# A reciprocal root moved from VectorE to GpSimd, and smaller first stores, in a two-layer decoder trunk

## The chip, the cores and the metric

The kernel runs on one core of one Trainium2 chip. Its engines work side by side, each through a queue of its own and in that queue's order: TensorE (PE) multiplies matrices, VectorE (DVE) and ScalarE (ACT) work elementwise, GpSimd (POOL) is a set of programmable cores, and SyncE (SP) issues transfers. Transfers between the core's SBUF and the chip's memory run on sixteen DMA engines. Matrix products land in PSUM, from where VectorE or ScalarE fetch them. The metric is the device time of one execution in microseconds (us), as the median of several runs.

## The reference

The model is a causal decoder trunk with two layers, 256 positions and a width of 2048, all in float32. Layer 0 mixes positions with eight stick-breaking heads and eight dilated-window heads, layer 1 with sixteen forgetting-attention heads. Each layer then has a gated feed-forward block with a depthwise convolution of width three (5632 columns per half), and a gated per-layer embedding. What matters here is the norm, which stands ahead of each mixer, of each feed-forward block and of each gate, and once more at the end, seven in all:

```python
def rmsnorm(x, g):
    x32 = x.astype(jnp.float32)
    y = x32 * lax.rsqrt(jnp.mean(x32 * x32, axis=-1, keepdims=True) + RMS_EPS)
    return (y * g.astype(jnp.float32)).astype(x.dtype)

def reference(...):
    h = x
    for i in range(DEPTH):
        a = rmsnorm(h, attn_norm[i])
        ...  # h = h + mixer(a)
        h = h + conv_ffn(rmsnorm(h, ffn_norm[i]), w_up[i], conv_w[i], conv_b[i], w_down[i])
        gate = jax.nn.sigmoid(rmsnorm(h, ple_norm[i]) @ w_ple_gate[i])
        h = h + gate * (p[i] @ w_ple[i])
    return rmsnorm(h, final_norm)
```

So for each of the 256 positions one number is needed, the reciprocal root of the mean square over 2048 features.

## The kernel before

The hidden state `h` stays in SBUF, features on the 128 partitions: 16 blocks of 128 features by 256 positions. Activations are held as two float32r parts (a rounded value and its rest), and so are the weights. A weight product is three matmuls (`PARTS`: high by high, high by low, low by high). Weights stream in from memory in groups of up to 1 MB over SyncE's queue (`issue_group`, L149) into three raw buffers. `split_unit` makes the two parts of one unit: ScalarE rounds (L165), VectorE subtracts (L166). Four such split buffers exist, and `LOOK = 3` units are kept ready ahead of TensorE. A unit is typically 4 blocks of 128 by 256 columns, 24 matmuls.

A counter of units used, the tick, orders what is done beside the matmuls: `defer(n, fn)` puts `fn` off until n units later. `norm_finish` defers `norm_sums` by 3 ticks and `norm_rows` by 5, so that two units of matmuls stand between them in TensorE's queue. What uses the norm's rows is put off until then as well (`with_rows`). The order within each engine's queue is finally laid out by a planner when the program is built: it takes the order of the program as the priority and its own estimates of durations, and may put a ready instruction ahead of one that waits. So in the profile a weight subtraction (L166) can stand among the small operations of a norm.

The norm works in three steps:

1. As each block of `h` is final, its squares are added up into `acc` (L278 to L282).
2. `norm_sums`: the two halves of `acc` are added (L287), four tiny matmuls with a vector of ones sum over the partitions (L291, into `nps`), with positions now on the partitions, two columns of 128. VectorE scales by 1/2048 and adds epsilon (`nv`, L296). Then come twelve operations on 128x2 values (L298 to L306): the reciprocal root by a shift of the bits, a subtraction from a constant, and three Newton steps. The last one writes `rT`.
3. `norm_rows`: `rT` is put on the diagonal of two 128x128 matrices (`nd`, L314, one VectorE operation for each column), which are split into two parts (`ndh` on ScalarE, L321; `ndl` on VectorE, L322) and multiplied with ones by TensorE (`rps`, L324), so that each partition gets the row of 256 roots. VectorE copies it to `rb` (L325), and to `rq` with the attention's scale where a mixer follows.

The columns are applied after the products: an attention's queries and keys, the feed-forward's up-products and the gate's product are multiplied by `rb` or `rq` when they are fetched from PSUM. Values use `rT` as a scale per position.

The seventh norm has no product behind it. The last gate column's product is made in two halves (L716) with their squares in `more` (L727); then come `norm_sums(more)`, `norm_rows(None)`, which multiplies in full float32 without the split (L316), eight products of `h` with the row (L739, 512 columns each, the second operand in PSUM) and, behind each one, a store of 256 KB on SyncE's queue (L740).

GpSimd has nearly nothing to do: four fills that the framework puts at the start and four small loads (the gains `gn` at L359, and L383 to L385).

## Time and profile before

| | before |
|---|---|
| median of 3 runs | 2437.97 us (2437.55 to 2438.04) |
| the profiled execution's own time | 2438.14 us |
| its span (first to last instruction) | 2436.3 us |
| granted TensorE clock, mean | 0.997 of full |
| TensorE busy | 2414.1 us, 99% |
| VectorE busy | 1595.7 us, 65% |
| ScalarE busy | 1228.3 us, 50% |
| GpSimd busy | 2.5 us |
| read from and written to memory | 452.86 MB, 2.10 MB |

Times in the views count from the start of the span. A row of the timeline or of the chain of waits gives start, duration, engine, line and operation, with the output ahead of the arrow and the inputs behind it; x8 means that eight alike are merged, and the brackets at the end of a timeline row hold the engine's idle time before it and what ended that. A row of a grouped view gives the busy time of the group, the mean duration of one in nanoseconds, and the idle time ahead of the group. A row of a table by stretches gives the stretch, the busy time of the five engines, the granted TensorE clock, the DMA engines' busy share and GB/s.

### The profile page before, as it was taken

The numbers are of one execution on the slowest core, as the hardware profiler recorded it, in microseconds if no ns is written. First come the engines' busy times: TensorE is split into PE (matmuls) and PEld (weight loads), VectorE is DVE, ScalarE is ACT, GpSimd is POOL, SyncE is SP. The second block draws the span as 40 slices with busy tenths as digits, with TensorE's granted clock in tenths as the row PEclk, the third lists the DMA queues.
The fourth block names the chain that finished last, engine by engine and source line by source line (L and its number), as shares of the span: only waits on it lengthen the run. The fifth ranks groups of instructions, "written<-read, shape, count | busy, mean of one in ns | idle before, by whom it ended". The sixth has DMA issues, their size and how long they took to land.

```text
span 2436.3 us, 48002 instructions
## 1 busy us (share of the span) xinstructions
PE 2414.1 (99%) x20990; PEld 2400.5 (99%) x20990; DVE 1595.7 (65%) x2157; ACT 1228.3 (50%) x1548; POOL 2.5 (0%) x8
## 2 busy tenths in 40 slices
PE   8999999999999999999999999999999999999997
PEld 8999999999999999999999999999999999999997
DVE  7557666776567657767765555677765776567676
ACT  6554455555355445555554444555543554455553
POOL 0000000000000000000000000000000000000000
PEclk9999999999999999999999999999999999999998
DMA  7444445555555555555554444555555555555553
GB/s 268 169 177 173 169 177 191 194 197 198 190 191 192 188 208 190 191 185 203 187 184 170 165 169 165 190 191 192 195 198 194 191 192 189 203 195 186 189 198 120
DMA packets 66483, 458.06 MB, mean 188 GB/s; under 512 B 7408, under 2 KB 7424, under 8 KB 16608
## 3 DMA queue, kind: packets, MB, share of 16 engines
q1 hardware_dynamic: 66096, 454.53, 52.8%
q8 instruction: 164, 2.69, 0.4%
q0 software_dynamic: 176, 0.46, 0.1%
q14 instruction: 47, 0.39, 0.0%
HBM read 452.86 MB, written 2.10 MB: 187 GB/s over the span
## 4 chain that ended last, share of the span: by engine, by line
PE 97%; DVE 1%; DMA 1%; ACT 1%; issue 0%; SPq 0%; DVEq 0%; ACTq 0%
PE psu L203 39%; PE psd L203 20%; PE pso L203 7%; PE psk L203 7%; PE psv L237 7%; PE psq L203 7%; PE psg L203 7%; DMA wr<-in_w 1%; PE avp L520 1%; PE psp L203 0%; PE pse L716 0%; PE scs L469 0%; PE psv L250 0%; PE sps L511 0%; PE avp L522 0%; PE scs L467 0%
## 5 line engine op out<-in xcount | busy, mean ns | idle before, releaser
L166 DVE TENSOR_TENSOR w<-wr,w 128x1024 fp32r<-128x1024 f32 (+2 forms) x882 | 1051.4, 1193 | 701.2 <-ACT w L165 695.5
L165 ACT CAST w<-wr 128x1024 fp32r<-128x1024 f32 (+2 forms) x882 | 905.6, 1028 | 1082.5 <-PE psu L203 355.1
L203 PE MATMUL psu<-act,w 128*128 128x256 f32 x8448 | 959.3, 276 | 0.0
L203 PEld LDWEIGHTS psu<-act,w 128*128 128x128 f32 x8448 | 958.3, 188 | 0.0
L203 PE MATMUL psd<-act,w 128*128 128x256 f32 x4224 | 479.7, 276 | 0.0
L203 PEld LDWEIGHTS psd<-act,w 128*128 128x128 f32 x4224 | 479.2, 188 | 0.0
L203 PE MATMUL psq<-act,w 128*128 128x256 f32 x1536 | 185.2, 279 | 1.2 <-DVE w L166 1.0
L203 PEld LDWEIGHTS psq<-act,w 128*128 128x128 f32 x1536 | 179.8, 188 | 2.1 <-DVE w L166 1.5
L203 PE MATMUL psk<-act,w 128*128 128x256 f32 x1536 | 180.0, 277 | 0.0
L203 PEld LDWEIGHTS psk<-act,w 128*128 128x128 f32 x1536 | 176.7, 188 | 0.0
L203 PE MATMUL pso<-act,w 128*128 128x256 f32 x1536 | 175.8, 277 | 0.0
L203 PEld LDWEIGHTS pso<-act,w 128*128 128x128 f32 x1536 | 174.9, 188 | 0.0
L237 PE MATMUL psv<-w,act 128*128 128x256 f32 x1440 | 172.7, 279 | 0.0
L237 PEld LDWEIGHTS psv<-w,act 128*128 128x128 f32 x1440 | 168.4, 188 | 1.1
L203 PE MATMUL psg<-act,w 128*128 128x256 f32 x1440 | 164.4, 276 | 0.0
L203 PEld LDWEIGHTS psg<-act,w 128*128 128x128 f32 x1440 | 163.7, 188 | 0.0
L616 DVE TENSOR_TENSOR u<-psu,rb 128x512 f32<-128x512 f32 x88 | 60.8, 691 | 33.3 <-PE psu L203 33.2
L622 DVE SCALAR_TENSOR_TENSOR yg<-u,cv,yg 128x256 f32<-128x256 f32 x176 | 73.3, 477 | 0.0
L622 DVE SCALAR_TENSOR_TENSOR yv<-u,cv,yv 128x256 f32<-128x256 f32 x176 | 73.3, 477 | 0.0
L619 ACT ACTIVATE yg<-u,cv 128x256 f32<-128x256 f32 x88 | 48.0, 594 | 1.0 <-DVE u L616 1.0
L619 ACT ACTIVATE yv<-u,cv 128x256 f32<-128x256 f32 x88 | 48.0, 593 | 0.0
L261 ACT CAST act<-yg 128x512 fp32r<-128x512 f32 x44 | 27.3, 621 | 39.1 <-DVE yg L632 39.1
(173 smaller groups left out, 886.5 us busy)
## 6 DMA issues: line engine op xcount, KB each, us to landing
wr<-in_w SPq DMA_DIRECT2D x388, 1024.0 KB, 4.8
wr<-in_w SPq DMA_DIRECT2D x36, 768.0 KB, 4.3
wr<-in_w SPq DMA_DIRECT2D x8, 896.0 KB, 4.6
wr<-in_w SPq DMA_DIRECT2D x7, 512.0 KB, 6.9
h<-in_x SPq DMA_DIRECT2D x4, 512.0 KB, 7.1
out_dram<-h SPq DMA_DIRECT2D x8, 256.0 KB, 2.4
wr<-in_w SPq DMA_DIRECT2D x2, 816.0 KB, 4.6
ct<-in_c SPq DMA_DIRECT2D x1, 841.0 KB, 6.6
```

The source lines that it names most:

```text
L165: nc.scalar.copy(out=w[:, :, 0, :], in_=raw)
L166: nc.vector.tensor_sub(out=w[:, :, 1, :], in0=raw, in1=w[:, :, 0, :].bitcast(F32))
L203: nc.tensor.matmul(ps[:, j, :], lhsT=w[:, k, s, js], rhs=act[:, k0 - koff + k, t, :], start=first and j + k + n == 0, stop=last and k == k ...
L237: nc.tensor.matmul(ps[:, t], lhsT=act[:, 4 * i + k, a, tsl], rhs=w[:, k, b], start=i + t + k + n == 0, stop=i == 3 and k == kc - 1 and n = ...
L261: nc.scalar.copy(out=dst[:, :, 0, :], in_=src)
L520: nc.tensor.matmul(av[:, 0, j * S:(j + 1) * S], lhsT=v[:, 0, js], rhs=w[:, j * S:(j + 1) * S], start=j == 0, stop=False, skip_group_check= ...
L616: nc.vector.tensor_mul(out=u[:, :, 2:], in0=ps, in1=rb2)
L619: nc.scalar.activation(out=y[:, j, :], in_=u[:, j, 2:], func=AF.Identity, bias=cv[:, l, t, 3:4], scale=cv[:, l, t, 2:3])
L622: nc.vector.scalar_tensor_tensor(out=y[:, j, :], in0=u[:, j, tap:tap + S], scalar=cv[:, l, t, tap:tap + 1], in1=y[:, j, :], op0=ALU.mult, ...
```

## The change

Three edits. The twelve operations behind `nv` become one instruction on GpSimd, a power with the exponent -0.5, which lies in a small constant tile that GpSimd fills at the start. In `norm_rows`, the second of the two diagonal matrices is made by ScalarE, as a copy with a scale, where VectorE made both. And the eight products and stores at the end become nine: two of one block (256 columns, 128 KB), then seven of two blocks (512 columns, 256 KB).

```diff
+    root = cpool.tile([P, 2], F32, name="root")
+    nc.gpsimd.memset(root, -0.5)
...
         v = work.tile([P, 2], F32, name="nv", tag="nv")
-        y = work.tile([P, 2], I32, name="ny", tag="ny")
-        t = work.tile([P, 2], F32, name="nt", tag="nt")
         nc.vector.tensor_scalar(out=v, in0=ps[:, :, 0], scalar1=1.0 / D, scalar2=EPS,
                                 op0=ALU.mult, op1=ALU.add)
-        nc.vector.tensor_single_scalar(out=y, in_=v.bitcast(I32), scalar=1, op=ALU.logical_shift_right)
-        nc.vector.tensor_scalar(out=y, in0=y, scalar1=-1.0, scalar2=float(0x5F3759DF),
-                                op0=ALU.mult, op1=ALU.add)
-        nc.vector.tensor_scalar_mul(out=v, in0=v, scalar1=-0.5)
-        y = y.bitcast(F32)
-        for i in range(3):
-            nc.vector.tensor_mul(out=t, in0=y, in1=y)
-            nc.vector.tensor_mul(out=t, in0=t, in1=v)
-            nc.vector.scalar_tensor_tensor(out=rT if i == 2 else y, in0=t, scalar=1.5, in1=y,
-                                           op0=ALU.add, op1=ALU.mult)
+        nc.gpsimd.tensor_tensor(out=rT, in0=v, in1=root, op=ALU.pow)
...
         for t in range(2):
-            nc.vector.tensor_scalar_mul(out=dg[:, t, :], in0=ident, scalar1=rT[:, t:t + 1])
+            if t == 0:
+                nc.vector.tensor_scalar_mul(out=dg[:, t, :], in0=ident, scalar1=rT[:, t:t + 1])
+            else:
+                nc.scalar.activation(out=dg[:, t, :], in_=ident, func=AF.Copy, scale=rT[:, t:t + 1])
...
-    rps = norm_rows(None).unsqueeze(1).to_broadcast([P, 2, S])
-    for op in range(8):
-        hs = h[:, 2 * op:2 * op + 2, :]
-        nc.vector.tensor_mul(out=hs, in0=hs, in1=rps)
-        nc.sync.dma_start(out=out[:, 2 * op:2 * op + 2, :], in_=hs)
+    rps = norm_rows(None)
+    for k0, k1 in ((0, 1), (1, 2), *((k, k + 2) for k in range(2, KT, 2))):
+        hs = h[:, k0:k1, :]
+        nc.vector.tensor_mul(out=hs, in0=hs, in1=rps.unsqueeze(1).to_broadcast([P, k1 - k0, S]))
+        nc.sync.dma_start(out=out[:, k0:k1, :], in_=hs)
```

## The prediction

> **What bounds the kernel now.** I read the first page first: busy shares, then the chain that ended last.
>
> ```profile
> span 2436.3 us, 48002 instructions
> PE 2414.1 (99%) x20990; PEld 2400.5 (99%) x20990; DVE 1595.7 (65%) x2157; ACT 1228.3 (50%) x1548; POOL 2.5 (0%) x8
> ...
> PE 97%; DVE 1%; DMA 1%; ACT 1%; issue 0%; SPq 0%; DVEq 0%; ACTq 0%
> ```
>
> TensorE is busy for 2414.1 of 2436.3 us, so 22.2 us are all that an edit beside the matmuls can touch. VectorE's 65% is not a limit: taking operations from it pays only where TensorE, or the end, waits for one of them. Two views find such places. The chain of waits, narrowed to the last microseconds, shows the seventh norm, behind which no matmul hides anything:
>
> ```profile
> 2422.98 0.62 PE nps L291 x4
> ...
> 2423.62 0.17 DVE nv L296
> ...
> 2423.82 0.18 DVE ny L298
> ...
> 2425.79 0.17 DVE rT L306
> ...
> 2425.98 0.30 DVE nd L314
> ...
> 2426.32 1.23 PE rps L316 x4
> ...
> 2427.58 0.69 DVE h L739
> ```
>
> From the end of `nv` (2423.62 + 0.17 = 2423.79) to the start of `nd` (2425.98) the chain is twelve small VectorE operations one behind the other: 2.19 us, all on the path that sets the end.
>
> For the six other norms I took TensorE's instructions grouped by line, whose last column is the idle time ahead of the group, and then the timeline of the first norm:
>
> ```profile
> L324 PE MATMUL rps<-ndh,trir 128*128 128x256 f32 x6 | 1.9, 313 | 1.0 <-ACT ndh L321 1.0
> ```
>
> ```profile
> 36.41 6.13 PE L203 MATMUL psk<-act,w 128*128 128x256 f32 x50
> ...
> 38.04 0.15 DVE L296 TENSOR_SCALAR nv<-nps 128x2 f32<-128x2 f32 x1
> ...
> 42.23 0.16 DVE L306 SCALAR_TENSOR_TENSOR rT<-nt,ny 128x2 f32<-128x2 f32 x1
> 42.42 0.48 DVE L314 TENSOR_SCALAR nd<-ct,rT 128x128 f32<-128x128 f32 x2
> ...
> 42.94 0.40 ACT L321 CAST ndh<-nd 128x256 fp32r<-128x256 f32 x1 [0.96 <-DVE nd L314]
> ...
> 43.40 0.39 PE L324 MATMUL rps<-ndh,trir 128*128 128x256 f32 x1 [0.86 <-ACT ndh L321]
> ```
>
> The six together let TensorE wait 1.0 us, and 0.86 of it is the first norm: TensorE was through with its keys at 42.54 (36.41 + 6.13) and got `ndh` at 43.40. The fourth norm has the rest, and the third stands for those without a wait:
>
> ```profile
> 1219.66 4.36 PE L250 MATMUL psv<-w,act 128*128 128x272 f32 x33
> 1219.84 0.16 DVE L296 TENSOR_SCALAR nv<-nps 128x2 f32<-128x2 f32 x1 [0.70 <-PE nps L291]
> ...
> 1224.20 0.39 PE L324 MATMUL rps<-ndh,trir 128*128 128x256 f32 x1 [0.17 <-ACT ndh L321]
> ```
>
> ```profile
> 1133.25 0.16 DVE L296 TENSOR_SCALAR nv<-nps 128x2 f32<-128x2 f32 x1 [0.70 <-PE nps L291]
> ...
> 1138.62 0.28 PE L324 MATMUL rps<-ndh,trir 128*128 128x256 f32 x1
> ```
>
> There the root has 5.2 us between `nv` (1133.41) and the row matmul, which stands two weight units later in TensorE's queue. So the change can win at three places only: 2.19 us at the end, 0.86 and 0.17 in the middle.
>
> **The power itself.** It takes the place of twelve operations seven times, and one wait of VectorE on itself becomes a wait for GpSimd and one back. The trace has no arithmetic on GpSimd; the nearest rows are these, with an exponential of ScalarE for the function:
>
> ```profile
> L359 POOL DMA_DIRECT2D gn<-in_g x1 | 0.7, 668 | 0.8 <-POOLq L809 0.8
> ...
> L809 POOL MEMSET const-float32-1.0<- 128x1 f32 x1 | 0.1, 98 | 0.0
> ```
>
> ```profile
> 1227.67 1.28 ACT L541 ACT_TABLE_LOAD   x1
> ...
> 1228.96 0.23 ACT L541 ACTIVATE fe<-fe 128x32 f32<-128x32 f32 x1
> ```
>
> Low end: a fill, 0.10 us. High end: a function whose tables must first come in, 1.28 + 0.23 = 1.51 us. I take 0.67, the row of GpSimd that is a routine of many steps. The two handoffs I set at 0.04 each, the gap that the tail shows between VectorE and TensorE (2425.98 + 0.30 to 2426.32). So `nv`'s end to `nd`'s start becomes 0.67 + 0.08 = 0.75 us, between 0.18 and 1.59. At the end that is 0.75 - 2.19 = -1.44 us (between -2.01 and -0.60).
>
> The Trainium skill, GPSIMD Engine Reference, section "Performance versus the Vector engine", speaks against moving elementwise work there: it gives 4497 ns against VectorE's 2293 ns for a two-input addition of 2048 columns, 1.96 times as long. VectorE's operations here are 0.17 us long with their gap, so an estimate by that ratio is 0.33 us for one of them on GpSimd, 0.41 with handoffs, and the end would win 1.78 instead of 1.44; no run here shows it, and that page's operation is an addition, not a power.
>
> In the first norm the power starts at 38.19 (38.04 + 0.15) and `rT` is there near 38.9. From `rT` to the row matmul it takes 0.30 (`nd`) + 0.02 + 0.40 (`ndh`) + 0.04 = 0.76 us, so TensorE's 42.54 is met with over two microseconds to spare, room for one weight cast or subtraction that the planner may place ahead (they are why the old chain took 4.2 us there, not 2.2). The wait goes: -0.86 us, between -0.86 and 0. The fourth likewise: -0.17, or 0. TensorE is without a break from there on, so these reach the end. In the other four the root is early already: 0. **Middle: -1.03 us.** The VectorE time set free (12 x 6 operations) buys nothing more, as no other row of TensorE waits for it.
>
> **The second `nd` on ScalarE.** It lies between the 0.23 us of 128x32 above and the 0.40 of `ndh`'s 128x256. In the tail TensorE asks for it only when the first half's passes are through, half of 1.23 us after 2426.32; it would be ready about 0.4 us behind `rT`, before that. Worth 0, with the first half's matmuls as cover; without it, at most its 0.40. In the middle norms `ndh` and weight casts stand behind it in ScalarE's queue; they shift by under 0.4 us, and the weights are two to three units ahead. ScalarE needs no table for the copy with a scale: in the tail it follows a sigmoid with none between.
>
> ```profile
> 2421.14 0.42 ACT L723 ACTIVATE gt<-gt 128x256 f32<-128x256 f32 x1 [3.10 <-DVE gt L722]
> ...
> 2422.96 0.51 ACT L686 ACTIVATE h<-h,gn 128x256 f32<-128x256 f32 x1 [1.41 <-DVE sq L727]
> ```
>
> **The fill of `root`** goes ahead of the four loads on GpSimd's queue: 0.10 us later for the gains (`gn`), first read by ScalarE at 12.96, over 10 us later: 0; uncovered it is 0.1.
>
> ```profile
> 12.96 0.21 ACT act L269
> ```
>
> **The stores.** Nine in place of eight; the first two are half as large. What counts is when the sixteen DMA engines can run without a break:
>
> ```profile
> L739 DVE TENSOR_TENSOR h<-h,rps x8: 677/679/687, 2427.6 to 2431.8; 128x512 f32<-128x512 f32 x8
> ```
>
> ```profile
> 2428.30 4.51 SPq L740 DMA_DIRECT2D out_dram<-h  x8
> ```
>
> ```profile
> 2429.10:2429.20 0.10, 0.00 (x0) 0.00 (x0) 0.10 (x1) 0.00 (x0) 0.00 (x0) 0.50 0.43 164
> ...
> 2434.60:2434.70 0.10, 0.00 (x0) 0.00 (x0) 0.00 (x0) 0.00 (x0) 0.00 (x0) 0.50 0.52 185
> ```
>
> ```profile
> 2420.68 0.42 DVE L722 TENSOR_TENSOR gt<-pse,rb 128x256 f32<-128x256 f32 x1 [3.19 <-PE pse L716]
> ```
>
> The second number from the right is the DMA share. The engines start at 2429.16 (0.43 of a tenth), 0.86 us after the first issue, and end at 2434.65: 5.49 us, 0.69 a piece. Products come 0.60 us apart (4.2 / 7) and last 0.68. Counted from the first product's start: the first bytes move at 0.69 + 0.03 + 0.86 = 1.58, and 8 x 0.686 later, at 7.07, it is over; the second piece was ready at 2.15, just ahead of the first one's end at 2.27. After the change the halves last 0.42 and come some 0.34 apart (0.42 less the overlap of 0.08 that the full ones show). Bytes move at 1.31, but the third piece, the first full one, has its product from 0.68 to 1.36 and its bytes at 2.25. The two halves are through by 2.0, the engines stand still, and seven full pieces end at 2.25 + 4.80 = 7.05. Gain 0.02; with halves 0.30 apart 0.10, and with small packets slower nothing. **Stores: 0**, between -0.1 and +0.1: the hole moves from ahead of the first piece to ahead of the third.
>
> **The sum.** -1.44 - 1.03 + 0 = -2.47 us on the profiled execution's own 2438.14, that is 2435.67. That execution lies 0.17 above the median of the runs (2437.97), so for the median **2435.5 us**. One unknown more: the last row matmuls ran at half clock.
>
> ```profile
> 2423.80:2423.90 0.10, 0.00 (x0) 0.00 (x0) 0.08 (x1) 0.00 (x0) 0.00 (x0) 0.89 0.00 0
> 2423.90:2424.00 0.10, 0.00 (x0) 0.00 (x0) 0.09 (x1) 0.00 (x0) 0.00 (x0) 0.50 0.00 0
> ```
>
> The granted clock falls at 2423.9; the new row matmuls would start near 2424.9 (2423.79 + 0.75 + 0.30 + 0.04), still behind it: 0. If the fall came later against the work, half of their 1.23 us would go: -0.6 as a low end.
>
> **Rivals.**
> 1. *The middle gains nothing.* The queues of VectorE and ScalarE are laid out anew, a cast or subtraction stands ahead of `nd` or `ndh`, and TensorE waits as before. For it: that happened to the twelve operations. Against: two microseconds to spare. Then -1.44 alone: 2436.5.
> 2. *The first power is slow, its code having to come from memory.* The profile's first page gives 4.8 us from issue to landing for a weight load:
>
> ```profile
> wr<-in_w SPq DMA_DIRECT2D x388, 1024.0 KB, 4.8
> ```
>
>    With it the first power takes 5.55 us, `rps` moves to 38.19 + 5.55 + 0.76 = 44.50, a loss of 1.10 in place of a gain of 0.86: -1.44 - 0.17 + 1.10 = -0.5, 2437.5. GpSimd's loads at the start show no such pause, but they are no arithmetic. (The Trainium skill, GPSIMD Engine Reference, section "Instruction dispatch", gives about 6 us for the first call of a freshly loaded kernel; by an estimate with its 5.95 the loss grows by 1.2. No run here shows it.)
> 3. *Slower: the power is long every time.* GpSimd works it out step by step. If a logarithm and an exponential cost as many steps as the thirteen operations from `nv` to `rT` each, 26 steps for each of two columns at the fill's 0.098 us, it takes 5.1 us, 5.2 with handoffs. The tail then loses 3.0. `rps` comes 38.19 + 5.18 + 0.76 = 44.13 in the first norm (+0.73), 1225.94 in the fourth (+1.74), 1139.35 in the third (+0.73) and so in its three likes: 3.0 + 0.73 + 1.74 + 4 x 0.73 = +8.4, 2446.3. It decides from 3.2 us on, where the tail's loss of 1.0 eats the middle's gain. Against it: the rows of GpSimd that exist are all under 0.7 us.
>
> **How the numbers follow.** The forecast has 0.68; its own range is 2434.2 (-2.01 - 1.03 - 0.6 - 0.1 = -3.74) to 2437.5 (-0.60 + 0.1). Rival 1 has 0.12, rival 2 0.07, rival 3 0.12 (0.05 of it beyond 4.7 us a power, where seven delays add up to 4.9 us); 0.01 is left for what I don't see. The range given goes from 2434.2 to 2438.6, which takes in rival 2 and a power of up to 3.2 us. By 0.2%, 4.9 us, which is about what a measurement can tell from no change, only the far part of rival 3 is slower (0.05), and faster would need more than the three places hold (2.19 + 1.03 + 0.6 + 0.1 = 3.9): 0.02. The same: 0.93.
>
> **What would show it.** On GpSimd seven powers; in the tail `nv`'s end to `nd`'s start near 0.75 us; no wait of TensorE ahead of `rps` in norms one and four; first store bytes 1.3 us after the first product's start, a dip of DMA share before the third piece, and the last bytes 7.05 us after that start. It is wrong if a power takes over 1.6 us, if TensorE waits for a norm anywhere, or if the stores end 0.2 us sooner than reckoned.

## The result, and the profile after

The kernel became slower: a median of 2524.17 us (2523.74 to 2524.98) against 2437.93 us (2437.55 to 2438.04) for the kernel before on the same chip, a ratio of 1.0355 [1.0343, 1.0367]. The forecast was 2435.5.

The first page of the profile of the changed kernel (own time 2524.54 us, mean granted clock 0.998):

```profile
span 2522.8 us, 47934 instructions
...
PE 2502.7 (99%) x20990; PEld 2490.2 (99%) x20990; DVE 1583.7 (63%) x2067; ACT 1229.4 (49%) x1555; POOL 8.3 (0%) x16
```

TensorE ran as many matmuls as before, 20,990, at the same mean clock (0.997 before), and was busy for 2502.7 us in place of 2414.1: 88.6 us more. The rest of the span, in which TensorE is not busy, went from 22.2 to 20.1 us (2522.8 - 2502.7), 2.1 less. So the part of the span that the prediction worked on became shorter, by about what was forecast (2.47), and the whole loss sits in a part that it took as fixed: 88.6 us over 20,990 matmuls are 4.2 ns for each.

The share of busy time is 99% in both kernels and shows nothing of this. The view that does is TensorE's largest group with its count (busy time of the group, then the mean duration of one). Before:

```profile
L203 PE MATMUL psu<-act,w 128*128 128x256 f32 x8448 | 959.3, 276 | 0.0
```

After:

```profile
L206 PE MATMUL psu<-act,w 128*128 128x256 f32 x8448 | 998.6, 280 | 0.0
```

The duration of one hardly differs, since matmuls overlap: each lasts about 276 ns, and the next one starts long before its end. Busy time over count is the pace: 959.3 / 8448 = 113.6 ns, then 998.6 / 8448 = 118.2. The same in the table by stretches, 100 us of each layer's feed-forward block and 100 us of the second layer's attention, before:

```profile
460.00:560.00 100.00, 100.00 (x885) 100.00 (x884) 71.06 (x100) 53.48 (x64) 0.00 (x0) 1.00 0.55 198
1400.00:1500.00 100.00, 100.00 (x841) 97.39 (x841) 54.75 (x75) 46.29 (x72) 0.00 (x0) 1.00 0.50 169
1660.00:1760.00 100.00, 100.00 (x885) 100.00 (x884) 72.91 (x105) 53.86 (x65) 0.00 (x0) 1.00 0.54 191
```

and after:

```profile
460.00:560.00 100.00, 100.00 (x845) 100.00 (x844) 69.98 (x100) 51.42 (x62) 0.00 (x0) 1.00 0.53 188
1400.00:1500.00 100.00, 100.00 (x813) 97.04 (x812) 52.02 (x73) 43.11 (x69) 0.00 (x0) 1.00 0.47 163
1660.00:1760.00 100.00, 100.00 (x853) 100.00 (x852) 68.63 (x97) 52.93 (x65) 0.69 (x1) 1.00 0.53 189
```

At full clock (the 1.00), with TensorE never idle, 885 matmuls fit into 100 us of the feed-forward blocks before and 845 or 853 after; in the attention it is 841 and 813. GpSimd does nothing at all in the first of these stretches, and the DMA engines move less, not more. So the new instructions are absent there, and yet the matmuls are slower.

What the prediction did look at can be read off as well. The seven powers, and the chain of waits in the last microseconds, after:

```profile
L299 POOL TENSOR_TENSOR rT<-nv,root x7: 688/690/1549, 36.8 to 2511.7; 128x2 f32<-128x2 f32 x7
```

```profile
2511.39 0.17 DVE nv L297
...
2511.67 0.72 POOLq L808
...
2512.42 0.30 DVE nd L307
...
2512.76 1.24 PE rps L311 x4
...
2514.02 0.42 DVE h L734
```

A power takes 0.69 us, the first one 1.55. From `nv`'s end (2511.56) to `nd` (2512.42) it is now 0.86 us in place of 2.19. The first norm in the timeline, after:

```profile
35.98 3.33 PE L206 MATMUL psk<-act,w 128*128 128x256 f32 x26
...
36.81 1.55 POOL L299 TENSOR_TENSOR rT<-nv,root 128x2 f32<-128x2 f32 x1 [33.23 <-DVE nv L297]
38.40 0.40 ACT L309 ACTIVATE nd<-ct,rT 128x128 f32<-128x128 f32 x1 [3.15 <-POOL rT L299]
38.71 1.03 ACT L168 CAST w<-wr 128x1024 fp32r<-128x1024 f32 x1
39.64 0.40 ACT L316 CAST ndh<-nd 128x256 fp32r<-128x256 f32 x1
...
40.09 0.39 PE L319 MATMUL rps<-ndh,trir 128*128 128x256 f32 x1 [0.79 <-ACT ndh L316]
```

A weight cast of 1.03 us stands between `nd` and `ndh` in ScalarE's queue, and only 26 matmuls, not 50, stand between the sums (`nps`) and the row matmul in TensorE's: it still waits for 0.79 us. That is all that the six norms cost, in the group of row matmuls, after:

```profile
L319 PE MATMUL rps<-ndh,trir 128*128 128x256 f32 x6 | 1.8, 297 | 0.8 <-ACT ndh L316 0.8
```

The stores, by stretches of the end, after:

```profile
2515.20:2515.40 0.20, 0.00 (x0) 0.00 (x0) 0.20 (x2) 0.00 (x0) 0.00 (x0) 0.50 0.28 97
2515.40:2515.60 0.20, 0.00 (x0) 0.00 (x0) 0.20 (x1) 0.00 (x0) 0.00 (x0) 0.50 1.03 348
2515.60:2515.80 0.20, 0.00 (x0) 0.00 (x0) 0.20 (x1) 0.00 (x0) 0.00 (x0) 0.50 0.65 210
...
2516.20:2516.40 0.20, 0.00 (x0) 0.00 (x0) 0.20 (x1) 0.00 (x0) 0.00 (x0) 0.50 0.67 241
...
2521.00:2521.20 0.20, 0.00 (x0) 0.00 (x0) 0.00 (x0) 0.00 (x0) 0.00 (x0) 0.50 0.59 215
```

First bytes near 2515.34 (0.28 of a fifth), 1.32 us behind the first product's start at 2514.02; last bytes near 2521.12 (0.59 of a fifth), 7.10 behind it. In between the DMA share dips twice, to 0.65 and 0.67.

### The profile page after: what moved, and what is told of

Same layout as the page of the kernel before. It is cut to its first block, busy times and chain, and to the rows that moved or that the text cites. A ratio compares the mean times of both kernels' runs of the same rounds, so it can differ in the third digit from the quotient of the medians.

```text
span 2522.8 us, 47934 instructions
## 1 busy us (share of the span) xinstructions
PE 2502.7 (99%) x20990; PEld 2490.2 (99%) x20990; DVE 1583.7 (63%) x2067; ACT 1229.4 (49%) x1555; POOL 8.3 (0%) x16
## 4 chain that ended last, share of the span: by engine, by line
PE 98%; DVE 1%; ACT 0%; issue 0%; DMA 0%; SPq 0%; POOL 0%; POOLq 0%; DVEq 0%
PE psu L206 40%; PE psd L206 20%; PE pso L206 7%; PE psk L206 7%; PE psv L240 7%; PE psq L206 7%; PE psg L206 7%; PE avp L515 1%; PE psv L253 0%; PE psp L206 0%; PE pse L711 0%; PE scs L464 0%; DMA wr<-in_w 0%; PE sps L506 0%; PE avp L517 0%
## 5 line engine op out<-in xcount | busy, mean ns | idle before, releaser
L206 PE MATMUL psu<-act,w 128*128 128x256 f32 x8448 | 998.6, 280 | 0.0
L206 PEld LDWEIGHTS psu<-act,w 128*128 128x128 f32 x8448 | 997.5, 188 | 0.0
L206 PE MATMUL psd<-act,w 128*128 128x256 f32 x4224 | 499.4, 280 | 0.0
L206 PEld LDWEIGHTS psd<-act,w 128*128 128x128 f32 x4224 | 498.9, 188 | 0.0
L206 PE MATMUL psk<-act,w 128*128 128x256 f32 x1536 | 186.2, 281 | 0.0
L206 PE MATMUL pso<-act,w 128*128 128x256 f32 x1536 | 182.6, 281 | 0.0
L206 PEld LDWEIGHTS pso<-act,w 128*128 128x128 f32 x1536 | 181.7, 188 | 0.0
L240 PE MATMUL psv<-w,act 128*128 128x256 f32 x1440 | 179.4, 283 | 0.0
L240 PEld LDWEIGHTS psv<-w,act 128*128 128x128 f32 x1440 | 175.0, 188 | 1.1
L272 ACT ACTIVATE act<-h,gn 128x256 fp32r<-128x256 f32 x96 | 43.5, 503 | 2.3 <-DMA h<-in_x 1.1
```

What stands on the lines that cost most here:

```text
L206: nc.tensor.matmul(ps[:, j, :], lhsT=w[:, k, s, js], rhs=act[:, k0 - koff + k, t, :], start=first and j + k + n == 0, stop=last and k == k ...
L240: nc.tensor.matmul(ps[:, t], lhsT=act[:, 4 * i + k, a, tsl], rhs=w[:, k, b], start=i + t + k + n == 0, stop=i == 3 and k == kc - 1 and n = ...
L272: nc.scalar.activation(out=dst[:, k, 0, :], in_=h[:, k, :], func=AF.Copy, scale=gn[:, g, k:k + 1])
```

## The experiments

If the matmuls are slower where none of the new instructions runs, something lasting must differ. The theories:

- **A, places.** `root` is a tile of 8 bytes per partition, which takes a slot of 32. It lies ahead of the four split weight buffers, so these move by 32 bytes (163008 to 163040 per partition, in the built kernels), while the activations stay where they were (32896 and 65664). In every weight product one operand is loaded into the array and the other streamed through it; one comes from the split weights, the other from the activations.
- **B, GpSimd.** Its arithmetic disturbs TensorE.
- **C, the order.** The planner's new order makes TensorE slower.
- **D, the new instructions' timing** in the middle norms.

Later, **R** is A made precise: what counts is the distance of split weights from activations, modulo some power of two; **S** is its rival: the place of the split weights alone counts. The *distance* below is the address of the first split weight buffer less that of the first activation buffer, per partition, modulo 256 bytes; it is the same for every pair, as the split weight buffers lie 8192 bytes apart, those of the activations 32768, and the blocks within them a multiple of 256. Before it is 64, after 96.

Ratios are to the kernel before, run on the same chip. Where a kernel made from the one before needs room for a slot, the tiles `nv`, `ny` and `nt` are parts of one tile `small`. The working tiles behind them, which hold the attention's scores and what is made of them, then lie 64 bytes lower against the working tiles ahead of them (queries, keys and values among these); split weights and activations do not move by it. This is not shown in the diffs.

### A slot without its use

The kernel before, and a tile of 8 bytes behind `rT` that GpSimd fills once and nobody reads. Distance 96.

```diff
     rT = cpool.tile([P, 2], F32, name="rT")
+    slot = cpool.tile([P, 2], F32, name="slot")
+    nc.gpsimd.memset(slot, -0.5)
```

> The kernel before, with its twelve VectorE operations, both diagonal matrices on VectorE and eight stores, and with one thing of the change alone: an unused constant tile of 8 bytes per partition behind rT, filled once by GpSimd. It takes a slot of 32 bytes, and all that is allocated behind it, the raw weights, the split weights and the working tiles, moves up by 32 bytes per partition: the split weights from 163008 (a multiple of 64) to 163040. (Room for it is made by putting the three tiny tiles of the root into one.) Theory A, places: matmuls that read split weights 32 bytes off a multiple of 64 take longer, so TensorE's start-to-start goes from 113.3 ns to 117 to 119 ns as in the changed kernel, and the time is that of the changed kernel without its shorter tail, about 2525.5 us. Rival B, GpSimd's arithmetic slows TensorE: no power here, 2438 us. Rival C, the planner's new order: the order is that of before, 2438 us.

2527.70 us (2526.05 to 2535.87), ratio 1.0377 [1.0361, 1.0394]. The two feed-forward stretches:

```profile
460.00:560.00 100.00, 100.00 (x855) 100.00 (x854) 70.77 (x100) 51.43 (x62) 0.00 (x0) 1.00 0.52 189
1660.00:1760.00 100.00, 100.00 (x845) 100.00 (x844) 68.30 (x107) 51.27 (x62) 0.00 (x0) 1.00 0.52 187
```

No power, no copy on ScalarE, eight stores: and all of the loss. B, C and D fall as its cause. The two paces, 855 and 845 in 100 us, are the changed kernel's (845 and 853), only in the other order of the layers.

### The whole change without the slot

The changed kernel, with the exponent in spare bytes of `rT`'s slot. Distance 64; as `ny` and `nt` are gone, the working tiles behind them (the attention's scores) lie 64 bytes lower than before. Nothing else moved.

```diff
-    rT = cpool.tile([P, 2], F32, name="rT")
-    root = cpool.tile([P, 2], F32, name="root")
+    rT = cpool.tile([P, 4], F32, name="rT")
+    root = rT[:, 2:4]
```

> The whole change, but the exponent -0.5 lies in columns 2 and 3 of the tile rT, whose slot of 32 bytes has room for it. So no tile in front of the split weights is added and they stay at 163008. Theory A: TensorE's start-to-start is back at 113.3 ns; the time is what the prediction summed from the tail and the first norms, 2435.5 to 2436.5 us, 1.5 to 2.4 us under before. Rivals B and C: as the changed kernel, about 2524 us.

2445.43 us (2444.57 to 2446.16), ratio 1.0032 [1.0019, 1.0044]. The 88 us are gone, but it is not the forecast's 2435.5. The stretches show why:

```profile
460.00:560.00 100.00, 100.00 (x885) 100.00 (x884) 71.21 (x100) 52.93 (x65) 0.00 (x0) 1.00 0.54 196
1400.00:1500.00 100.00, 100.00 (x821) 97.03 (x820) 52.94 (x72) 44.59 (x70) 0.00 (x0) 1.00 0.49 172
```

The feed-forward is at the old pace. In the second layer's attention 821 matmuls fit, where before it was 841. In the trace the weight matmuls there start 117.4 ns apart from about 1280 us to about 1640, where the next norm breaks the stream, and 113.3 ns apart behind it. So a slow pace can also set in within one attention, at distance 64, and end at the next break in the stream.

### The slot in two other places

First between the raw and the split weight buffers, so that the split ones move and the raw ones don't. Distance 96.

```diff
+    slot = wpool.tile([P, 2], F32, name="slot")
+    nc.gpsimd.memset(slot, -0.5)
```

> The kernel before with the same unused 32-byte slot, now between the raw weight buffers and the split ones: the raw buffers stay where they were, the split weights and the working tiles move by 32 bytes. Theory A with the split weights as the cause: as the slot in front of both, about 2525.5 us. If the raw buffers were the cause (transfers or ScalarE and VectorE reading them): 2438 us. Rivals B and C: 2438 us.

2534.32 us (2524.84 to 2535.60), ratio 1.0388 [1.0373, 1.0404]; 845 matmuls in 100 us:

```profile
460.00:560.00 100.00, 100.00 (x845) 100.00 (x845) 69.42 (x99) 51.68 (x63) 0.00 (x0) 1.00 0.50 182
```

The raw buffers, and with them the transfers from memory, have no part in it. Then behind the split weights, in a pool of its own, where only working tiles move. Distance 64.

```diff
+    lpool = ctx.enter_context(tc.tile_pool(name="lpool", bufs=1))
...
+    slot = lpool.tile([P, 2], F32, name="slot")
+    nc.gpsimd.memset(slot, -0.5)
```

> The kernel before with the same slot behind the split weights: only the working tiles (queries, keys, values, norm and feed-forward temporaries) move by 32 bytes. Theory A with the split weights as the cause: 2438 us, within 1 us of before; attention's own small matmuls may change by some nanoseconds each. If the working tiles were the cause: about 2525 us.

2446.97 us (2445.98 to 2447.48), ratio 1.0038 [1.0024, 1.0052]; 885 matmuls in the feed-forward stretch, and a stretch of 117 ns from about 80 to 430 us, this time in the first layer's attention. So moving the split weights brings the large loss, and moving the working tiles some 9 us.

### The whole change with every place kept

As the second experiment, and one unused tile of 64 bytes where `ny` and `nt` were, so that all tiles lie as before.

```diff
-    root = cpool.tile([P, 2], F32, name="root")
+    rT = cpool.tile([P, 4], F32, name="rT")
+    root = rT[:, 2:4]
...
+        if not padded:
+            padded.append(work.tile([P, 16], F32, name="pad", tag="pad"))
+            nc.gpsimd.memset(padded[0], 0.0)
```

> The whole change, with the exponent in the spare bytes of rT's slot and with an unused 64-byte tile where the two tiny integer and float tiles of the root had been. So the split weights and also the attention's and feed-forward's working tiles stand exactly where they stood before. Theory A, places (the split weights off a multiple of 64 cost 86 us, and the 64 bytes by which the working tiles moved in the run with the exponent in rT cost the other 9 in layer 1's attention): TensorE's start-to-start as before, 2435.5 to 2436.5 us, the prediction's own sum. Rival D, the power, the copy on ScalarE or the new stores bring TensorE into its slow pace in layer 1's attention by their timing: about 2445 us again, with 117 to 118 ns between 1280 and 1640 us.

2435.85 us (2434.91 to 2436.47, 11 runs), ratio 0.9993 [0.9984, 1.0002]: 0.35 us from the forecast. The attention's stretch, the group of row matmuls, and a row of the tail's chain:

```profile
1400.00:1500.00 100.00, 100.00 (x845) 97.85 (x845) 54.77 (x75) 46.29 (x72) 0.00 (x0) 1.00 0.49 172
```

```profile
L322 PE MATMUL rps<-ndh,trir 128*128 128x256 f32 x6 | 1.8, 296 | 0.8 <-ACT ndh L319 0.8
```

```profile
2423.65 0.73 PE rps L314 x4
```

The attention has its pace back. The first norm's wait is there (0.8), as in the changed kernel, and the tail's row matmuls happened to run before the clock fell, in 0.73 us where the changed kernel's took 1.24.

### The activations moved too, and a larger slot

To part R from S: 32 bytes ahead of the activations and 32 more ahead of the split weights, which then lie at a multiple of 64 once more (163072). Distance 96.

```diff
+    slot = cpool.tile([P, 2], F32, name="slot")
+    nc.gpsimd.memset(slot, -0.5)
     bufs = [cpool.tile([P, KT, 2, S], F32R, name=f"act{i}") for i in range(2)]
+    slot2 = cpool.tile([P, 2], F32, name="slot2")
+    nc.gpsimd.memset(slot2, -0.5)
```

> The kernel before, with the two activation buffers moved up by 32 bytes (one unused 32-byte slot in front of them) and a second slot behind them, so that the split weights stay on a multiple of 64 (163072, 64 bytes further than before). If what counts is that either operand of a matmul starts off a multiple of 64: 117 to 119 ns and about 2525 us. If only the split weights count (they are the stationary operand of all products but the values'): 113.3 ns outside of attention and 2438 to 2447 us; the values' products, where activations are stationary, then go to about 120 ns as they do in the changed kernel.

2515.94 us (2515.39 to 2525.05), ratio 1.0331 [1.0315, 1.0346]. And the changed kernel with a `root` of 64 bytes: split weights at 163072 again, activations in place. Distance 128.

```diff
-    root = cpool.tile([P, 2], F32, name="root")
+    root = cpool.tile([P, 16], F32, name="root")
```

> The changed kernel with 64 bytes for the exponent's tile in place of 8 (which take 32): everything behind it moves by 64, the split weights to 163072. If a multiple of 64 is what the weights need: 113.3 ns in the feed-forward stages and 2435 to 2447 us, by how attention falls. If they need to stand at 64 beyond a multiple of 128 (as before) or any other finer place: 117 to 119 ns and about 2524 us. Rivals B and C (GpSimd's arithmetic, the order) have no reason for another time than 2524.

2537.93 us (2536.96 to 2538.58), ratio 1.0413 [1.0397, 1.0429]:

```profile
460.00:560.00 100.00, 100.00 (x845) 100.00 (x844) 69.62 (x99) 51.66 (x63) 0.00 (x0) 1.00 0.53 190
```

Both are slow. It isn't enough that the split weights lie at a multiple of 64; nor is it enough that the distance is a multiple of 64, for 128 is one too.

### The power alone

The power, with all places kept; `nd` on VectorE twice, eight stores.

```diff
-        nc.vector.tensor_single_scalar(out=y, in_=v.bitcast(I32), scalar=1, op=ALU.logical_shift_right)
...
+        nc.gpsimd.tensor_tensor(out=rT[:, 0:2], in0=v, in1=root, op=ALU.pow)
```

> The power alone, with all places as before: both diagonal matrices on VectorE and eight stores as before. Prediction's terms: -1.3 us at the end (the power measured 0.69 us, with its handoffs 0.86 from nv to nd against 2.19) and up to -1.0 us at the first and fourth norm: 2435.6 us. The copy on ScalarE and the halved stores have 0 in the sum, so this run and the one with the whole change should agree within 0.5 us. Rival: the halved first stores win by themselves, then this run lies 0.3 us or more above the whole change.

2434.88 us (2434.03 to 2436.26, 11 runs), ratio 0.9989 [0.9980, 0.9998]. TensorE hardly waits for a norm any more, 0.1 us in all six:

```profile
L319 PE MATMUL rps<-ndh,trir 128*128 128x256 f32 x6 | 1.8, 296 | 0.1
```

The first norm of this run beside that of the changed kernel shows why:

```profile
37.57 3.32 PE L206 MATMUL psk<-act,w 128*128 128x256 f32 x27
...
39.22 1.05 ACT L168 CAST w<-wr 128x1024 fp32r<-128x1024 f32 x1 [2.36 <-PE psk L206]
39.99 0.48 DVE L309 TENSOR_SCALAR nd<-ct,rT 128x128 f32<-128x128 f32 x2 [0.61 <-POOL rT L302]
...
40.51 0.41 ACT L316 CAST ndh<-nd 128x256 fp32r<-128x256 f32 x1 [0.23 <-DVE nd L309]
```

The matmuls that cover it are 27 here and 26 there. But ScalarE has no copy to wait for, so the weight cast runs while the power is still at work, ahead of `ndh` without delaying it; in the changed kernel the cast stood behind the copy and so between `nd` and `ndh`.

### Four places for the activations

All four are the kernel before with something put ahead of the activations. First the small tile `bft` (a slot of 64 bytes): split weights where they were, activations 64 higher. Distance 0.

```diff
+    bft = cpool.tile([P, NH], F32, name="bft")
     bufs = [cpool.tile([P, KT, 2, S], F32R, name=f"act{i}") for i in range(2)]
...
-    bft = cpool.tile([P, NH], F32, name="bft")
```

> The kernel before with one allocation in another place: the 64-byte tile of the forget bias stands ahead of the activation buffers, not behind the constants, so the activations begin 64 bytes further (32960 in place of 32896) and the split weights and all working tiles are where they were (163008). Split weights minus activations, modulo 128, goes from 64 to 0, the value of the slow run with a 64-byte slot. Theory R, the distance of a matmul's two operands decides (64 modulo 128 is fast, all else slow): 117 to 119 ns, about 2516 to 2538 us. Theory S, the place of the split weights alone decides (64 modulo 128 is fast): 113.3 ns, about 2438 us.

2564.11 us (2564.09 to 2564.97), ratio 1.0519 [1.0503, 1.0535], the slowest of all:

```profile
460.00:560.00 100.00, 100.00 (x836) 100.00 (x835) 66.37 (x93) 49.91 (x60) 0.00 (x0) 1.00 0.50 187
```

S falls: the split weights have not moved by a byte. (The tiles between the two operands moved by 64 as well; the move by 512 below answers that.) Then a slot of 64 bytes ahead of the activations, so that both move by 64 (distance 64), and the same with 32 bytes (`[P, 2]`), so that the split weights lie at 163040 as in the changed kernel (distance 64).

```diff
+    slot = cpool.tile([P, 16], F32, name="slot")
+    nc.gpsimd.memset(slot, -0.5)
     bufs = [cpool.tile([P, KT, 2, S], F32R, name=f"act{i}") for i in range(2)]
```

> The kernel before with a 64-byte slot ahead of the activations: activations, split weights and working tiles up to the small ones all stand 64 bytes further, so the distance of the operands is as before and the split weights stand at a multiple of 128 (163072), where the run with the 64-byte slot behind rT took 2537.9 us. Theory R: 113.3 ns in the feed-forward stages and 2436 to 2447 us. Theory S: 118.7 ns, about 2538 us.

> The kernel before with a 32-byte slot ahead of the activations: activations and split weights both stand 32 bytes further, neither on a multiple of 64 (32928, 163040), with their distance as before. Theory R: 113.3 ns in the feed-forward stages, 2436 to 2447 us. Theory S, and any rule that asks for a multiple of 64: 117 to 119 ns, about 2525 us, as the changed kernel with its split weights at 163040.

2446.57 us (2446.32 to 2448.62), ratio 1.0038 [1.0024, 1.0052], and 2447.11 us (2446.94 to 2447.50), ratio 1.0039 [1.0024, 1.0054]. The stretch of the second one:

```profile
460.00:560.00 100.00, 100.00 (x885) 100.00 (x884) 70.95 (x101) 53.86 (x65) 0.00 (x0) 1.00 0.53 198
```

The split weights lie where the changed kernel has them, and the pace is the fast one: the place itself is harmless, the distance counts. The 9 us that remain are again a slow stretch of 117.4 ns in the second layer's attention. In both runs the attention's score tiles lie 64 bytes lower against the queries, keys and values, as in the second experiment, where they alone moved, and as in the run with the slot behind the split weights. Last, a tile of 128 bytes (`cq`) ahead of the activations. Distance 192.

```diff
+    cq_odd = cpool.tile([P, 2, NH], F32, name="cq_1")
     bufs = [cpool.tile([P, KT, 2, S], F32R, name=f"act{i}") for i in range(2)]
...
-        cq = cpool.tile([P, 2, NH], F32, name=f"cq_{l}")
+        cq = cq_odd
```

> The kernel before with the 128-byte tile of the gates' sums allocated ahead of the activations: these stand 128 bytes further (33024), the split weights where they were. The distance is 64 modulo 128 still, but 192 in place of 64 modulo 256. Theory R with a period of 128, and theory S: 113.3 ns, 2436 to 2447 us. Theory R with a period of 256: 117 to 119 ns, 2516 us or more.

2513.37 us (2508.84 to 2513.85), ratio 1.0306 [1.0291, 1.0321]. Slow in both feed-forward blocks (117.8 ns). But at the end of the second attention the same distance shows the fast pace: 708 matmuls in 80 us, 113.3 ns from start to start.

```profile
460.00:560.00 100.00, 100.00 (x851) 100.00 (x850) 69.15 (x97) 51.36 (x62) 0.00 (x0) 1.00 0.51 188
1580.00:1660.00 80.00, 80.00 (x708) 80.00 (x707) 51.85 (x61) 42.14 (x54) 0.00 (x0) 1.00 0.55 198
```

### Distance 32, a move by 512, and the two other edits alone

`rT` moved ahead of the activations, split weights in place. Distance 32. And `gn` (448 bytes) with `bft` (64) ahead, together 512. Distance 64.

```diff
+    rT = cpool.tile([P, 2], F32, name="rT")
     bufs = [cpool.tile([P, KT, 2, S], F32R, name=f"act{i}") for i in range(2)]
...
-    rT = cpool.tile([P, 2], F32, name="rT")
```

```diff
+    gn = cpool.tile([P, 7, KT], F32, name="gn")
+    bft = cpool.tile([P, NH], F32, name="bft")
     bufs = [cpool.tile([P, KT, 2, S], F32R, name=f"act{i}") for i in range(2)]
```

> The kernel before with the tile rT allocated ahead of the activations: these stand 32 bytes further, the split weights stay. The distance of the operands is 32 modulo 512; measured so far are 64 (113.3 ns), 96 (117.3 or 118.7), 128 (118.7), 0 (120.0) and 448 (117.8). Theory R says only that it is the distance that decides; if 64 is an isolated good place, 32 gives 115 to 120 ns and more than 2470 us; if there is a range of good places around it, 113.3 ns and 2438 to 2447 us.

> The kernel before with the gains (448 bytes) and the forget bias (64) allocated ahead of the activations, which so stand 512 bytes further; the split weights stay. The distance is 64 modulo 512 as before, but 576 modulo 1024. Since the products read both operands in steps of 512 bytes and more, theory R with a period of 512 or less expects 113.3 ns and 2436 to 2447 us; a longer period, 115 ns or more in the feed-forward stages.

2529.25 us (2528.54 to 2529.73), ratio 1.0376 [1.0360, 1.0392] for 32; 2437.64 us (2437.10 to 2438.41, 10 runs), ratio 1.0000 [0.9991, 1.0009] for the move by 512. It is the kernel before again to a tenth of a microsecond, so the rule has a period, and 512 is a multiple of it. In this run the convolution's taps, the constants and the rows that lie between the two operands moved by 64 bytes, exactly as with `bft` alone ahead of the activations (2564.11): so it was not these. The stretch at distance 32:

```profile
460.00:560.00 100.00, 100.00 (x848) 100.00 (x847) 69.64 (x99) 51.60 (x63) 0.00 (x0) 1.00 0.51 184
```

The copy on ScalarE alone, then the nine stores alone, both with all places kept:

```diff
-            nc.vector.tensor_scalar_mul(out=dg[:, t, :], in0=ident, scalar1=rT[:, t:t + 1])
+            if t == 0:
+                nc.vector.tensor_scalar_mul(out=dg[:, t, :], in0=ident, scalar1=rT[:, t:t + 1])
+            else:
+                nc.scalar.activation(out=dg[:, t, :], in_=ident, func=AF.Copy, scale=rT[:, t:t + 1])
```

> The copy on ScalarE alone: the kernel before, all places kept, the twelve VectorE operations and eight stores kept, only the second diagonal matrix made by ScalarE. Prediction: 0. From the run of the whole change with places kept (2435.85) against the power alone (2434.88), whose profiles show 0.8 and 0.1 us of waiting ahead of the first norm's row matmul: if the copy is what costs that 1 us, since the split ndh now stands behind it and a weight cast in ScalarE's queue, this run takes 0.3 to 1 us more than before; if it is the stores, this run is at 2437.9.

```diff
-    for op in range(8):
-        hs = h[:, 2 * op:2 * op + 2, :]
...
+    for k0, k1 in ((0, 1), (1, 2), *((k, k + 2) for k in range(2, KT, 2))):
+        hs = h[:, k0:k1, :]
```

> The nine stores alone: the kernel before, all places kept, with two half-size pieces first. Prediction: 0, between -0.1 and +0.1 us: the engines idle ahead of the third piece for what they gain ahead of the first. Rival: the sooner start is a gain of about 0.27 us in full, the first piece's product being 0.42 in place of 0.68 us long; or the ninth store's issue costs up to 0.3 us.

2437.45 us (2436.71 to 2438.26), ratio 1.0000 [0.9991, 1.0009], and 2437.47 us (2436.59 to 2438.09), ratio 0.9999 [0.9990, 1.0008], 11 runs each: both nothing. The nine stores leave the first norm as it was in the kernel before. Its group of row matmuls:

```profile
L324 PE MATMUL rps<-ndh,trir 128*128 128x256 f32 x6 | 1.9, 316 | 0.3 <-ACT ndh L321 0.2
```

The same norms with the same order cost 0.3 us here and 1.0 in the profile of before: that wait varies from one execution to the next.

### Is the period 512 or 256?

The power alone with `cv` (2816 bytes) ahead of the activations (distance 320 modulo 512, 64 modulo 256), and with `cv` and `bft` (256 modulo 512, 0 modulo 256).

```diff
+    cv = cpool.tile([P, DEPTH, 2 * FT, 4], F32, name="cv")
+    bft = cpool.tile([P, NH], F32, name="bft")
     bufs = [cpool.tile([P, KT, 2, S], F32R, name=f"act{i}") for i in range(2)]
```

> The same with the taps alone ahead of the activations: the distance is 320 modulo 512. As for 256: 113.3 ns and 2425 to 2435 us if the far side of the period is good; 117 ns or more and over 2500 us if 64 is isolated. A period of 256 instead of 512 would make this run fast (320 is 64 modulo 256) and the one at 256 slow (as 0).

> The power alone with places as before (2434.88 us when measured), but with the convolution's taps (2816 bytes) and the forget bias (64) allocated ahead of the activations: the distance of split weights and activations becomes 256 modulo 512; nothing behind the constants moves. Measured so far: 64 is fast, 0, 32, 96, 128 and 448 are slow. If the two operands disturb each other when they are near each other in the period of 512, the far side is good and 256 gives 113.3 ns, in attention too, and up to some us less than 2434.9; if 64 is an isolated good place, 117 ns or more and over 2500 us.

2434.43 us (2433.60 to 2435.83, 10 runs), ratio 0.9988 [0.9978, 0.9997], and 2564.25 us (2562.87 to 2564.34), ratio 1.0520 [1.0502, 1.0537]. The stretch of each:

```profile
460.00:560.00 100.00, 100.00 (x885) 100.00 (x883) 71.04 (x100) 53.52 (x65) 0.00 (x0) 1.00 0.55 199
460.00:560.00 100.00, 100.00 (x836) 100.00 (x835) 66.51 (x92) 49.51 (x60) 0.00 (x0) 1.00 0.52 188
```

885, the count of distance 64, and 836, the count of distance 0. At both distances a further 256 bytes change nothing; a further 128 do, as 64 is fast and 192 isn't. The period is 256, as far as these distances tell.

### What the runs give together

The third column is the mean time from the start of one weight matmul to that of the next in this stretch. It is a little longer than 100 us over the count, because the count takes in two or three matmuls that are under way when the stretch begins.

| distance mod 256 | matmuls in 460 to 560 us | ns from start to start | times (us) |
|---|---|---|---|
| 0 (two kernels) | 836, 836 | 120.0 | 2564.1, 2564.3 |
| 32 | 848 | 118.3 | 2529.3 |
| 64 (before and ten more) | 884 or 885 | 113.3 | 2434.4 to 2447.1 |
| 96 (after and three more) | 845 or 855 | 118.7 or 117.3 | 2515.9 to 2534.3 |
| 128 | 845 | 118.7 | 2537.9 |
| 192 | 851 | 117.8 | 2513.4 |

At distance 64, 2434.4 to 2437.9 are the kernel before and the six whose other places are kept, or that had tiles moved ahead of the activations; 2445.4 to 2447.1 are the four whose score tiles lie 64 bytes lower against the queries, keys and values, each with one attention at about 117 ns.

## Why the prediction was wrong

**The step that failed** is "The fill of `root`". It counted the instruction, 0.10 us on GpSimd's queue, and put the edit at 0; that the tile which is filled takes a place, and that everything behind it moves, was not considered. It measured about 88 us in place of 0 (2524.17 with the tile, 2435.85 without it and all places kept). This one declaration costs all that the change lost: without any of the rest it gave a ratio of 1.0377, and the whole change without it 0.9993. With it fell the sentence that the 22.2 us in which TensorE is idle "are all that an edit beside the matmuls can touch": the busy 2414.1 us were taken as fixed, and they hold 20,990 matmuls whose pace depends on where their operands lie. The range was built from the costs of instructions and waits, so no end of it could reach 2524, and none of the three rivals was this.

**The power.** The tail went from 2.19 us to 0.86 (forecast 0.75): 0.69 for the power, and 0.17 for both handoffs in place of 0.08. That the 0.67 taken from the row of a GpSimd load came so near was luck, as nothing ties a load's row to a power. Alone, with places kept, the power measured 2434.88 against 2437.56, -2.7 us, where tail and middle together were put at -2.47. Rival 3, a power that is long each time, is out. Rival 2 is there in small: the first power takes 0.86 us more than the others (1549 ns against 690), not 4.8; that its code is the reason is not shown. The Trainium skill, GPSIMD Engine Reference, section "Instruction dispatch", gives about 6 us for the first call of a freshly loaded kernel. The trace has no pause of that size here: the power begins 0.16 us behind `nv` (36.50 + 0.15 to 36.81) and lasts 1.55; whether its code was freshly loaded then, no run shows. One reading ahead was a little off, though nothing in the sum hangs on it: VectorE's operations with their gap take 0.18 us (2.19 over twelve), not 0.17.

**The middle.** In the changed kernel rival 1 held for the first norm, and with it the sign "if TensorE waits for a norm anywhere": a weight cast stood ahead of `ndh`, and the two microseconds to spare were gone, since the planner put the row matmul behind 26 matmuls in place of 50. So 0.79 of the 0.86 us stayed; the fourth norm's 0.17 went. With the power alone both went (0.1 left in all six). The term of 1.03 itself was one execution's value: the same order showed 0.3 elsewhere.

**The second `nd` on ScalarE.** Put at 0, and 0 when alone. Together with the power it is what brings the first norm's wait back: all four profiles that have both show 0.8 us, all three of the power without the copy 0.1 or less, and the stores come only at the end. What stands behind the copy in ScalarE's queue was put down as shifted by less than 0.4 us; that the 1.03 us cast would come between copy and `ndh` was not. In the median the whole change is 0.97 above the power alone (2435.85 against 2434.88); the two ratios' intervals overlap, so how much of that is the copy's stays open.

**The stores.** Put at 0: 2437.47 against 2437.60 alone. First bytes at 1.32 us (forecast 1.31), the dip ahead of the third piece is there (0.67 at 2516.2 to 2516.4, where 2.25 us behind the first product's start were reckoned, 2516.27), with one more between the two halves that I had not seen, the end at 7.10 (7.05).

**The clock.** The changed kernel's row matmuls took 1.24 us at half clock, as forecast; with all places kept the profiled execution had them in 0.73 before the fall, the gain of half a microsecond that the low end allowed for.

So for the change as instructions the direction was right and the size too large: with places kept it gave -1.71 us (2435.85 against 2437.56 on the same chip; the ratio's interval includes 1), where -2.47 was forecast. That 2435.85 lies so near to 2435.5 is in part luck: 0.41 us of it is the kernel before, which ran that much faster here than the forecast's 2437.97, and the first norm's wait did not go. The power alone, or with `cv` moved (2434.4 to 2434.9), is 0.1% faster than the kernel before.

**What stays open.** Shown is that the distance of the two operands decides on the pace of the feed-forward blocks, not how. The Trainium skill, TensorE: Matmul & The Clock Gate, section "Step-by-step: what each phase is for", says that TensorE has two independent read ports, one for the streamed operand and one for the load of the next weights, and that the load takes no bandwidth from the running matmul. By that rule alone one would expect no effect of the distance; 836 against 885 matmuls in 100 us differ from it. The distance isn't the whole rule either: 96 has two paces in one kernel, 64 a slow one of 117.4 ns in one attention, 192 a fast stretch of 80 us. Open is why, and which of the score tiles starts the slow pace in an attention (some 9 us). At 96 the runs of one kernel also lie up to 11 us apart (2524.84 to 2535.60). Distances of 160 and 224, and such as are no multiple of 32, weren't tried.

## What to carry to other kernels

Ask of each edit what it moves in memory, not only which instructions it adds: a constant of 8 bytes between the activations and the split weights cost 88 us here; in the spare bytes of another tile it cost nothing, and an unused tile of the same size ahead of both operands left the feed-forward blocks at their pace. After a small change that moves the time by per cents, compare the number of matmuls in equal stretches of both traces before reading any wait, since a busy share of 99% looks alike at both paces. Where a kernel is all matmuls, the distance of loaded from streamed operand, modulo 256 bytes, is a size to be tried on its own.

## What the runs showed of the hardware

- The pace of matmuls on float32r parts (128x128 by 256 columns, a new load for each) goes from 113.3 to 120.0 ns at full clock, in the feed-forward blocks, with the distance of their operands modulo 256 bytes; absolute places don't count there (both operands moved by 64 or by 32: 885 in 100 us, as before).
- At one and the same distance the pace can differ from one stage to the next: at 64, 117.4 ns over some 360 us of an attention in which only the score tiles had moved, and 113.3 behind the next norm; at 192, 117.8 in the feed-forward blocks and 113.3 over 80 us.
- A power on GpSimd of 128x2 values takes 0.69 us, the first one 1.55; from the end of its input's operation on VectorE to the start of the next one there, 0.86 us.
